# A router softmax on one NeuronCore: the late rows of x loaded in pairs instead of singly

## The chip, the cores and the metric

The kernel runs on one core of one Trainium2 chip. The metric is the time on the device in microseconds (us), the median of several executions. One execution was also taken by the hardware profiler; its span runs from the first to the last instruction or transfer that the profile shows and is a little shorter than the time of that execution.

## The reference

```
logits = matmul(x, router_weights)            # x: 16 x 512 x 1024 fp32, weights: 1024 x 8 fp32
exp_logits = exp(logits - max(logits, -1))    # per token, over 8 values
return exp_logits / sum(exp_logits, -1)       # 16 x 512 x 8 fp32
```

There are 16 x 512 = 8192 tokens of 1024 values each. Every token is multiplied with a 1024 x 8 matrix, and a softmax is taken over its 8 results. Reading x (33.6 MB in fp32) is by far the largest transfer; the output is 0.26 MB.

## The kernel before

The 8192 tokens are laid out as 128 partitions by 64 rows (`J = 64`): partition p holds tokens 64p to 64p+63, so one "row" j is one token in every partition, 128 tokens in all, and several neighbouring rows of one partition are contiguous in memory. A row of x is 128 x 1024 values, 512 KB in fp32.

**Loads.** `LOADS` (line 38) says how many rows each load brings: thirteen loads of four rows, three of two, five of one, which are rows 0 to 62. The first load goes through SyncE in fp32 and is cast by ScalarE. All others are issued by GpSimd (line 76) and cast from fp32 to bf16 on the way, each into a tile of its own, so no load waits for a buffer. The last row, 63, comes in two pieces (`LAST_LOADS = [6, 2]`, line 86): columns 0 to 767 and columns 768 to 1023. All loads issued by GpSimd share one DMA queue and are issued in the order of the rows.

**Work on a row.** The schedule is written out by hand: on each engine the instructions stand in the order of the program (`tc.manual_schedule()`).

- `turn` (line 155) transposes the row's eight 128 x 128 blocks on TensorE into PSUM (line 162). From row `NEAR = 54` on, five blocks go into one PSUM buffer and three into another. There are four such buffers (`psum_t`, line 49).
- `evict` (line 169) copies the transposed blocks to SBUF (line 173): up to row 53 VectorE copies all eight, from row 54 on VectorE copies five and ScalarE three.
- `project` (line 107) multiplies the row's eight blocks with the weights, eight matmuls that accumulate (line 114).
- `softmax` (line 124) puts five small steps on a list (`later`): `peak` (L134), `power` (L137 on VectorE and L140 on ScalarE), `total` (L143), `recip` (L146), `scale` (L149). `GROUPS` says which rows share one softmax; rows 54 to 61 are a group of eight. `step()` takes the next of the five from the list, one after each row.

**The loop** (line 182) runs over rows 0 to 61: it turns and evicts row j, takes one step of a softmax, and projects the row before it (from row 54 on). For rows 24 to 59 one or two filler matmuls (line 104) follow; rows 60 and 61 have none.

**The end** (lines 193 to 224) is written out. Row 61 is projected; the first two softmax steps of the group 54 to 61 run (`peak`, `power`); row 62 is turned and evicted; `total` runs; the two pieces of row 63 are turned, row 62 is projected, row 63 is evicted and projected, and a shared softmax of rows 62 and 63 ends in the last store (line 224):

```
        while pend:
            project(*pend.pop(0))
        step(2)
        xb, k = x_of[J - 2]
        before = evict(turn(xb[:, k, :], (5, 3)))
        step(1)
        (xa, ka, na), (xb, kb, nb) = x_last
        turned = turn(xa, (4, 2), ka) + turn(xb, (2, 0), kb)
        project(J - 2, before)
        last = evict(turned)
```

SyncE stores rows 0 to 53 of the output (line 195) after a tiny transfer (`mark`, line 194) that waits for the first piece of row 63.

Of the kernel before, what the change touches and what calls it, by code (L numbers as in the profile page):

```python
# [10 lines left out]
def kernel(  # L11
# [23 lines left out]
    ALU = mybir.AluOpType  # L35


    LOADS = [4] * 13 + [2, 2, 2] + [1] * 5
    LAST_LOADS = [6, 2]
    GROUPS = [8] * 6 + [6, 8, 1, 1]  # L40
    assert sum(LOADS) == J - 1 and sum(LAST_LOADS) == KO and sum(GROUPS) == J
    DONE = sum(GROUPS[:7])
# [11 lines left out]
    with tc.manual_schedule():  # L54
# [7 lines left out]

        x_f32 = const.tile([P, LOADS[0], D], fp32)
        for k in range(0, LOADS[0], 2):
            nc.sync.dma_start(out=x_f32[:, k:k + 2, :], in_=x_rows[:, k:k + 2, :])
# [3 lines left out]
        j0 = 0  # L69
        for i, r in enumerate(LOADS):  # L70
            xb = xpool.tile([P, r, D], bf16, name=f"x_{i}", tag=f"x_{i}")
# [183 lines left out]
```

## Time and profile before

| What | Value |
|---|---|
| time, median of 3 executions | 88.93 us (88.87 to 88.97) |
| the profiled execution | 88.78 us, its span 87.0 us |
| TensorE transposes and matmuls (PE) | busy 63.8 us, 73% of the span |
| VectorE (DVE) | busy 48.1 us, 55% |
| ScalarE (ACT) | busy 12.4 us, 14% |
| GpSimd (POOL), of which issuing loads 20 x 543 ns and 2 x 527 ns | busy 12.9 us, 15% |
| read from memory | 33.59 MB, written 0.26 MB |
| loads of four rows issued by GpSimd | 12, each 1024 KB as written in bf16 |
| loads of two rows | 3, each 512 KB |
| loads of one row | 5, each 256 KB |
| the pieces of the last row | 192 KB and 64 KB |

In the profile, PE is TensorE's matmuls and transposes, PEld its weight loads, DVE is VectorE, ACT is ScalarE, POOL is GpSimd, SP is SyncE. A line of the timeline reads: start in us from the span's start, duration in us, engine, source line, operation, output and input, number of instructions, and in brackets how long the engine had been idle and what ended that. A line of the chain of waits gives the shares of the span that the chain, followed back from the last instruction, spends on each kind of work. The ends of matmuls are modelled, so starts are read rather than ends where both are there. When GpSimd shows as idle until a DMA, it waits for an earlier load of its own to land before it issues the next.

### The profile page before, as it was taken

The page shows a single profiled execution, that of the slowest core. Times are in us where ns is not written, and L with a number is a line of the kernel's source. Part 1 is how long each engine was busy: PE and PEld are TensorE (multiplying, and loading weights), DVE is VectorE, ACT ScalarE, POOL GpSimd, SP SyncE. Part 2 cuts the span into 40 slices and gives each one's busy share as a digit, 9 for nine tenths or more (in the row PEclk, how much of TensorE's full clock was granted, in tenths as well). Part 3 has the DMA queues.
Part 4 walks back from the last instruction along what each step waited for, and adds up shares of the span by engine and source line. Part 5 has one row for each costly group of instructions (what it writes and reads, how often), then busy time and mean ns, then how long its engine had stood idle before and what let it go on. Part 6 is the DMA issues. An engine that isn't in the chain of part 4 may idle for free.

```text
span 87.0 us, 2427 instructions
## 1 busy us (share of the span) xinstructions
PE 63.8 (73%) x1092; PEld 53.6 (62%) x1092; DVE 48.1 (55%) x112; ACT 12.4 (14%) x25; POOL 12.9 (15%) x29
## 2 busy tenths in 40 slices
PE   0408004999396926949999998989898999997730
PEld 0407004999296926947777775757575888795620
DVE  0303300699576663723677677746676589563760
ACT  3235009000100010000010001000100003454540
POOL 5990002020010202020010202020010222000000
PEclk9999999999956999555999999999999999999997
DMA  3899999999999999999999999999999999999520
GB/s 60 328 358 286 260 249 222 222 211 230 196 222 211 222 215 211 226 207 215 218 215 226 200 226 215 207 226 207 226 207 198 220 213 210 202 210 211 88 102 19
DMA packets 3773, 18.26 MB, mean 210 GB/s; under 512 B 556, under 2 KB 940, under 8 KB 1972
## 3 DMA queue, kind: packets, MB, share of 16 engines
q0 software_dynamic: 3168, 15.73, 88.3%
q1 hardware_dynamic: 580, 2.36, 7.3%
q8 instruction: 8, 0.13, 0.5%
q10 hardware_dynamic: 16, 0.03, 0.2%
q14 instruction: 1, 0.01, 0.0%
HBM read 33.59 MB, written 0.26 MB: 389 GB/s over the span
## 4 chain that ended last, share of the span: by engine, by line
DMA 89%; POOL 3%; issue 2%; DVE 1%; PE 1%; ACT 0%; POOLq 0%
DMA x<-in_x_dram 75%; DMA xe<-in_x_dram 14%; POOL x L76 2%; POOL filler L81 1%; DVE xT L173 0%; PE lg L114 0%; PE pt L162 0%; POOL ident masks.py:199 0%; ACT ev_last L215 0%; POOL ident masks.py:197 0%; DVE ssum_last L219 0%; DVE low L214 0%; DVE ssum_last L220 0%; DVE outv L221 0%; POOLq L239 0%
## 5 line engine op out<-in xcount | busy, mean ns | idle before, releaser
L173 DVE COPY xT<-pt 128x1024 bf16<-128x1024 bf16 (+2 forms) x65 | 42.0, 652 | 31.8 <-PE pt L162 31.6
L162 PE MATMUL pt<-identity,x 128*128 128x128 bf16 x504 | 43.4, 236 | 16.0 <-ACT x L74 8.1
L162 PEld LDWEIGHTS <-x 128*128 128x128 bf16 x504 | 34.6, 105 | 25.8 <-DMA x<-in_x_dram 10.9
L114 PE MATMUL lg<-w_bf,xT 128*128 128x8 bf16 x512 | 22.7, 168 | 0.3 <-DVE xT L173 0.2
L114 PEld LDWEIGHTS <-xT 128*128 128x128 bf16 x512 | 20.7, 99 | 0.5 <-DVE xT L173 0.5
L104 PE MATMUL spare<-filler 128*128 128x512 bf16 x60 | 19.2, 384 | 0.0
L76 POOL DMA_DIRECT2D x<-in_x_dram x20 | 10.7, 543 | 56.2 <-DMA x<-in_x_dram 55.4
L140 ACT ACTIVATE ev<-ex 128x64 f32<-128x64 f32 (+1 forms) x8 | 2.0, 255 | 56.2 <-DVE ex L137 56.2
L173 ACT COPY xT<-pt 128x384 bf16<-128x384 bf16 (+1 forms) x10 | 4.7, 467 | 5.1 <-PE pt L162 4.9
L74 ACT CAST x<-x_f 128x1024 bf16<-128x1024 f32 x4 | 4.0, 1042 | 8.5 <-DMA x_f<-in_x_dram 8.5
L104 PEld LDWEIGHTS <-filler 128*128 128x128 bf16 x60 | 4.1, 96 | 0.0
L92 PE MATMUL lg<-ident,w 8*128 8x8 f32 x8 | 1.0, 254 | 3.1 <-POOL ident masks.py:199 3.1
L92 PEld LDWEIGHTS lg<-ident,w 8*128 8x128 f32 x8 | 1.0, 198 | 3.1 <-POOL ident masks.py:199 3.1
L89 DVE CAST identity<-ident 128x128 bf16<-128x128 f32 x1 | 0.5, 512 | 3.0 <-POOL ident masks.py:199 3.0
L134 DVE TENSOR_REDUCE mx<-lg 128x8 f32<-128x64 f32 (+1 forms) x8 | 1.7, 213 | 0.5 <-PE lg L114 0.5
L137 DVE TENSOR_TENSOR ex<-lg,mx 128x64 f32<-128x64 f32 (+1 forms) x8 | 1.7, 213 | 0.0
L149 DVE TENSOR_TENSOR outv<-ev,inv 128x64 f32<-128x64 f32 (+1 forms) x8 | 1.7, 212 | 0.0
L143 DVE TENSOR_REDUCE ssum<-ev 128x8 f32<-128x64 f32 (+1 forms) x8 | 1.7, 208 | 0.0
L86 POOL DMA_DIRECT2D xe<-in_x_dram x2 | 1.1, 527 | 3.9 <-DMA x<-in_x_dram 3.9
L146 DVE RECIPROCAL inv<-ssum 128x8 f32<-128x8 f32 (+1 forms) x8 | 1.5, 191 | 0.0
L74 ACT ACT_TABLE_LOAD x1 | 1.3, 1283 | 1.3 <-PEq L239 1.3
L162 PE MATMUL pt<-identity,xe 128*128 128x128 bf16 x8 | 0.6, 222 | 0.2 <-DMA xe<-in_x_dram 0.2
(14 smaller groups left out, 3.4 us busy)
## 6 DMA issues: line engine op xcount, KB each, us to landing
x<-in_x_dram POOLq DMA_DIRECT2D x12, 1024.0 KB, 35.4
x_f<-in_x_dram SPq DMA_DIRECT2D x2, 1024.0 KB, 8.4
x<-in_x_dram POOLq DMA_DIRECT2D x3, 512.0 KB, 33.9
x<-in_x_dram POOLq DMA_DIRECT2D x5, 256.0 KB, 20.6
out_dram<-outv SPq DMA_DIRECT2D x1, 216.0 KB, 1.9
xe<-in_x_dram POOLq DMA_DIRECT2D x1, 192.0 KB, 11.8
xe<-in_x_dram POOLq DMA_DIRECT2D x1, 64.0 KB, 9.7
out_dram<-outv SPq DMA_DIRECT2D x1, 40.0 KB, 1.5
```

The source lines that it names most:

```text
L74: nc.scalar.copy(xb[:, k, :], x_f32[:, k, :])
L76: nc.gpsimd.dma_start(out=xb[:], in_=x_rows[:, j0:j0 + r, :])
L92: nc.tensor.transpose(w_ps[:, n, :], w8[:, :, n], ident[0:KO, 0:KO])
L104: nc.tensor.matmul(spare[:], lhsT=filler[:, 0:P], rhs=filler[:], start=True, stop=True)
L114: nc.tensor.matmul(logits[g][:, k, :], lhsT=xT[:, i, :], rhs=w_bf[:, k0 + i, :], start=(k0 + i == 0), stop=(k0 + i == KO - 1),)
L134: nc.vector.reduce_max(mx[:, :, 0], lg, axis=X)
L137: nc.vector.tensor_tensor(out=ex[:], in0=lg, in1=mx[:].broadcast_to([P, n, N]), op=ALU.subtract)
L140: nc.scalar.activation(ev[:], ex[:], func=Exp)
L143: nc.vector.reduce_sum(ssum[:, :, 0], ev[:], axis=X)
L149: nc.vector.tensor_tensor(out=outv[:, a:a + n, :], in0=ev[:], in1=inv[:].broadcast_to([P, n, N]), op=ALU.mult)
L162: nc.tensor.transpose(pt[:, c, :], xb[:, (i + c) * P:(i + c + 1) * P], identity[:])
L173: copy(out=xT[:], in_=pt[:, 0:n, :])
```

## The change

The last eight loads of whole rows before, three of two rows and five of one, become six: five of two rows and one of one row. Rows 52 to 57 come in pairs as they did. Rows 58 and 59, which were two loads, are one; so are rows 60 and 61. Row 62 stays a load of its own, and row 63 stays in its two pieces.

```diff
-    LOADS = [4] * 13 + [2, 2, 2] + [1] * 5
+    LOADS = [4] * 13 + [2] * 5 + [1]
     LAST_LOADS = [6, 2]
     GROUPS = [8] * 6 + [6, 8, 1, 1]
```

GpSimd issues 20 loads instead of 22. The order of the instructions on TensorE, VectorE, ScalarE and SyncE is the same; four rows are read out of tiles that hold two rows.

## The prediction

> **What bounds the kernel now.** I read the page's slices first, then the chain of waits, then GpSimd's timeline for the pace of the loads, and last the timeline of the end, where the edit acts. From the page, the DMA row and the chain by line:
>
> ```profile
> DMA  3899999999999999999999999999999999999520
> ...
> DMA x<-in_x_dram 75%; DMA xe<-in_x_dram 14%; POOL x L76 2%; POOL filler L81 1%; DVE xT L173 0%; PE lg L114 0%; PE pt L162 0%; POOL ident masks.py:199 0%; ACT ev_last L215 0%; POOL ident masks.py:197 0%; DVE ssum_last L219 0%; DVE low L214 0%; DVE ssum_last L220 0%; DVE outv L221 0%; POOLq L239 0%
> ```
>
> The DMA engines are busy from the second slice to slice 37 of 40, and loads are 89% of the chain. So the time is the load stream plus what must be computed after its last piece. The stream's pace, from the timeline of GpSimd:
>
> ```profile
> 62.90 0.53 POOL L76 DMA_DIRECT2D x<-in_x_dram  x1 [4.37 <-DMA x<-in_x_dram]
> 67.81 0.53 POOL L76 DMA_DIRECT2D x<-in_x_dram  x1 [4.38 <-DMA x<-in_x_dram]
> 70.27 0.53 POOL L86 DMA_DIRECT2D xe<-in_x_dram  x1 [1.93 <-DMA x<-in_x_dram]
> 72.72 0.53 POOL L86 DMA_DIRECT2D xe<-in_x_dram  x1 [1.93 <-DMA x<-in_x_dram]
> ```
>
> GpSimd issues eight loads at once and then one for each that lands, so these starts are landings of the loads eight places earlier: 67.81 is the last load of four rows, 70.27 and 72.72 are the first two pairs. Four rows take 4.91 us, two rows 2.46 and 2.45. The last issue comes at 72.72, nearly 10 us before its data is used: the queue never runs dry.
>
> The end, from the timeline of all engines, 77.5 to 83.5 us:
>
> ```profile
> 77.45 0.57 PEld L162 LDWEIGHTS <-x 128*128 128x128 bf16 x8
> ...
> 77.97 0.31 PEld L114 LDWEIGHTS <-xT 128*128 128x128 bf16 x8
> ...
> 78.20 0.10 PEld L104 LDWEIGHTS <-filler 128*128 128x128 bf16 x1
> ...
> 78.70 0.45 PEld L162 LDWEIGHTS <-x 128*128 128x128 bf16 x8 [0.40 <-DMA x<-in_x_dram]
> ...
> 79.97 0.45 PEld L162 LDWEIGHTS <-x 128*128 128x128 bf16 x8 [0.56 <-DMA x<-in_x_dram]
> ...
> 80.38 0.31 PEld L114 LDWEIGHTS <-xT 128*128 128x128 bf16 x8
> ...
> 80.46 0.49 DVE L173 COPY xT<-pt 128x640 bf16<-128x640 bf16 x1 [0.78 <-PE pt L162]
> 80.69 0.48 ACT L173 COPY xT<-pt 128x384 bf16<-128x384 bf16 x1 [0.79 <-PE pt L162]
> 81.01 0.35 PEld L114 LDWEIGHTS <-xT 128*128 128x128 bf16 x8 [0.33 <-DVE xT L173]
> ...
> 81.28 0.46 PEld L162 LDWEIGHTS <-x 128*128 128x128 bf16 x8
> ...
> 81.49 0.23 DVE L134 TENSOR_REDUCE mx<-lg 128x8 f32<-128x64 f32 x1 [0.53 <-PE lg L114]
> ...
> 81.89 0.48 DVE L173 COPY xT<-pt 128x640 bf16<-128x640 bf16 x1
> 82.00 0.26 ACT L140 ACTIVATE ev<-ex 128x64 f32<-128x64 f32 x1 [0.84 <-DVE ex L137]
> ...
> 82.15 0.47 PEld L162 LDWEIGHTS <-xe 128*128 128x128 bf16 x8 [0.41 <-DMA xe<-in_x_dram]
> ...
> 82.17 0.91 ACT L173 COPY xT<-pt 128x384 bf16<-128x384 bf16 x2
> 82.29 0.22 DVE L143 TENSOR_REDUCE ssum<-ev 128x8 f32<-128x64 f32 x1
> ...
> 82.59 0.62 DVE L173 COPY xT<-pt 128x512 bf16<-128x512 bf16 x2
> ```
>
> Counting back from the end, the turns (L162) at 77.45, 78.70, 79.97, 81.28 and 82.15 are rows 59, 60, 61, 62 and 63. Rows 60 and 61 are waited for, 0.40 and 0.56 us, so their landings are 78.70 and 79.97. Two things then meet at 82.59. One is the last row: it lands at 82.15 and is turned. The other starts at row 61: its copy (80.46), its projection (81.01), then on VectorE `peak` (81.49), `power`, the copy of row 62 (81.89) and `total` (82.29 to 82.51), and only then the copy of row 63. That chain is done 0.08 us before it is needed. VectorE often starts an instruction about 0.08 before the one ahead of it ends by the profile (81.89 after an end at 82.37 gives 82.29), so the room is 0.08 to 0.16 us; I take 0.12. The page's chain names the load because it came last, but row 61 is almost level with it.
>
> **What the Trainium skill says.** "DMA: Bandwidth & Descriptors", section "Anatomy of one DMA", gives about 2.0 us fixed per DMA issued by GpSimd, mostly the wait for the receipt of the write. The trace agrees that it is no cost here: with eight in flight, single rows land every 1.25 us (74.97 to 79.97, four rows, below). The same page, section "Why a DMA increments its semaphore by 16 and not by 1", says that a load is complete only when all engines have posted; so neither row of a pair can be used until the whole pair lands. The trace shows it: rows 56 and 57 start at 74.97, after a wait for DMA, and 75.64, without one. "Perfetto Trace Analysis", section "DMA Optimizations", states both sides of the edit: larger transfers use the memory better, and splitting lets work start sooner. The trace has a size for each.
>
> **The change part by part.**
>
> *Two issues removed on GpSimd* (2 x 0.53 us), and the pieces of row 63 issued two places earlier: nothing, since the last issue before already lies some 9.4 us ahead of its landing, behind a full queue. The rest of GpSimd's queue is empty then. SyncE's `mark` still waits for the first piece of row 63, and its store of rows 0 to 53 only follows that piece: nothing.
>
> *The stream becomes a little faster.* From 74.97 (third pair landed) to 79.97 (row 61 landed) four single rows take 5.00 us. Two pairs at 2.455 take 4.91. So row 61 lands 0.09 us earlier, and so do rows 62 and 63. Bounds from the last two single rows, which took 2.52 (77.45 to 79.97), 0.065 more than a pair: 0.06 if only one pair gains that, 0.13 if both do.
>
> *Rows 58 and 59 arrive together* at about 77.45 - 0.05 = 77.40. TensorE is through with row 57 and its filler at about 76.50 and then idles. Two rows cost 0.87 us each with filler (rows in full flow at 69.10 and 69.97 start so), so it is free at about 79.15, before the next pair lands. Nothing, hidden by the wait for rows 60 and 61.
>
> *Rows 60 and 61 arrive together* at 79.97 - 0.09 = 79.88, and row 60's work, before done at 78.70 in the wait for row 61, now stands in front of row 61's. On TensorE that is the turn of row 60 and the projection of row 59: 0.41 us from the turn's first weight load to the projection's (79.97 to 80.38), and 0.23 us from the projection's first weight load to the next instruction (77.97 to 78.20). Bounds 0.64, and 0.71 if the projection's loads must end first (0.41 + 0.30); I take 0.66. VectorE (0.49 per copy) and ScalarE (0.48) keep up with that, and the four PSUM buffers hold exactly these two rows, so no other wait is added. Row 61's turn thus starts at 79.88 + 0.66 = 80.54 instead of 79.97: 0.57 late.
>
> *What is queued behind it.* Row 61's projection is followed in program order by row 62's turn on TensorE, which then starts at 81.85, when row 62 has been there since about 81.1 (79.97 + 1.25 - 0.09); by `peak` and `power` and row 62's copy on VectorE; by the exponential (82.00) and row 62's copy on ScalarE. All move by 0.57. Row 63's turn is no longer held by its load but by row 62's. Of the 0.57, the room of 0.12 at 82.59 is used up; the rest moves row 63's copy, its projection and the last softmax and store one for one.
>
> Sum against the profiled span: 87.0 + 0.66 - 0.09 - 0.12 = 87.45, that is +0.45 us. On the median of the runs, 88.93 (the profiled execution took 88.78, within 0.2% of it), it gives 89.38. With all bounds at one end it is 0.64 - 0.13 - 0.16 = +0.35 and 0.71 - 0.06 - 0.08 = +0.57.
>
> **The rivals.** A change of 0.2%, 0.18 us, is about what a measurement of this kernel can tell from none.
>
> *A: the stream alone sets the end.* If the row-61 chain has more room than I read, the time moves by the stream's gain: 88.93 - 0.09 = 88.84, no measurable change, the other side of my forecast. It decides when the room is at least 0.57 instead of 0.12. For it speaks that the chain of waits names the load; against it, that `total` ends 0.08 before the copy of row 63. A version of it that is faster by over 0.2% needs pairs to gain more than 0.18 us, over the 0.13 bound.
>
> *B: partial absorption.* Row 62's copies and row 63's overlap better when they come densely, and half of the delay is lost on the way: about +0.2, 89.13.
>
> *C: more is added.* If the second row of the pair costs a full row as in full flow (0.87, rows at 69.10 and 69.97), since its turn waits for copies or buffers, the sum is 0.87 - 0.09 - 0.12 = +0.66, 89.59. Against it: rows 60 and 61 have no filler.
>
> That the edit does not do what it says is out: the instruction order shows two loads fewer on GpSimd and the same order elsewhere.
>
> **How the numbers follow.** My forecast, 89.38 with 89.28 to 89.50 of its own, has 0.62; C 0.13, B 0.13 (half of it under the 0.2% line), A 0.12, of which a third is faster by over 0.2% with some luck in the runs. The range from 89.05 to 89.65 takes in most of B and C and leaves out A. Faster 0.04, within 0.2% 0.15 (0.08 of A and 0.07 of B), slower 0.81.
>
> **What would show it.** Right: TensorE's turn of row 60 near 79.9 with a wait for DMA ahead of it, row 61's turn about 0.65 later without one; `peak` of the last group near 82.05 instead of 81.49; the turn of row 63 no longer waiting for its load; the last store near 85.1 instead of 84.62; landings of pairs every 2.45 us to the end. Wrong: row 63's turn still waiting for its load at about 82.06 and the last store before 84.7 (A), or row 61's turn 0.87 after row 60's (C).

## The result, and the profile after

| | before | after |
|---|---|---|
| time, median | 88.91 us (88.74 to 88.97, 6 executions) | 89.12 us (89.04 to 89.27, 6 executions) |
| span of the profiled execution | 87.0 us | 87.5 us |

The ratio is 1.0029, with a 95% interval of 1.0016 to 1.0042: the changed kernel is slower, by 0.26 us (0.14 to 0.37); the two medians alone differ by 0.21. A second measurement gave 1.0032 (1.0020 to 1.0043), which is 0.28 us. The forecast was 0.45 us slower, so the direction is right and the size too large. The profiled execution of the changed kernel was the slowest of its six (89.27), that of the kernel before is below its median (88.78), so the two spans differ by more than the medians do.

The page of the changed kernel, its DMA row and the chain by line:

```profile
DMA  2999999999999999999999999999999999999220
...
DMA x<-in_x_dram 89%; PE lg L114 1%; PE pt L162 1%; DVE xT L173 1%; ACT ev_last L215 0%; DVE mx L134 0%; DVE ex L137 0%; DVE ssum_last L219 0%; DVE low L214 0%; DVE ssum_last L220 0%; DVE outv L221 0%; POOLq L239 0%
```

The stream is as busy as before, but the chain no longer ends with the pieces of row 63 (xe, 14% before). It runs over a load of whole rows and then over `peak` and `power` (L134, L137), which were not on it. The timeline of the end, all engines:

```profile
77.49 0.45 PEld L162 LDWEIGHTS <-x 128*128 128x128 bf16 x8 [0.84 <-DMA x<-in_x_dram]
...
78.16 0.65 PEld L162 LDWEIGHTS <-x 128*128 128x128 bf16 x8
...
79.95 0.45 PEld L162 LDWEIGHTS <-x 128*128 128x128 bf16 x8 [0.85 <-DMA x<-in_x_dram]
...
80.35 0.31 PEld L114 LDWEIGHTS <-xT 128*128 128x128 bf16 x8
...
80.44 0.49 DVE L173 COPY xT<-pt 128x640 bf16<-128x640 bf16 x1 [0.99 <-PE pt L162]
80.59 0.45 PEld L162 LDWEIGHTS <-x 128*128 128x128 bf16 x8
...
81.09 0.49 DVE L173 COPY xT<-pt 128x640 bf16<-128x640 bf16 x1 [0.16 <-PE pt L162]
...
81.63 0.35 PEld L114 LDWEIGHTS <-xT 128*128 128x128 bf16 x8 [0.30 <-DVE xT L173]
...
81.91 0.46 PEld L162 LDWEIGHTS <-x 128*128 128x128 bf16 x8
...
82.11 0.23 DVE L134 TENSOR_REDUCE mx<-lg 128x8 f32<-128x64 f32 x1 [0.53 <-PE lg L114]
82.15 0.71 SPq L194 DMA_DIRECT2D mark<-xe  x1
82.33 0.43 PEld L162 LDWEIGHTS <-xe 128*128 128x128 bf16 x7
...
82.92 0.22 DVE L143 TENSOR_REDUCE ssum<-ev 128x8 f32<-128x64 f32 x1
83.05 0.27 PE L162 MATMUL pt<-identity,xe 128*128 128x128 bf16 x2 [0.17 <-DVE xT L173]
...
83.06 0.61 DVE L173 COPY xT<-pt 128x512 bf16<-128x512 bf16 x2
...
85.07 0.34 SPq L224 DMA_DIRECT2D out_dram<-outv  x1
```

The turns at 77.49, 78.16, 79.95, 80.59, 81.91 and 82.33 are rows 58 to 63. Each pair is waited for once: the first row has a wait for DMA, the second has none. Row 60's turn starts where row 61's did (79.95, before 79.97), and row 61's follows 0.64 us later. `peak` starts at 82.11 instead of 81.49. SyncE's `mark` shows when the first piece of row 63 is there: 82.15, before 82.13. Yet row 63's weight loads, at 82.33, no longer name a wait for it. The last store starts at 85.07 instead of 84.62. The two lines of the kernel before:

```profile
82.13 0.70 SPq L194 DMA_DIRECT2D mark<-xe  x1
...
84.62 0.34 SPq L224 DMA_DIRECT2D out_dram<-outv  x1
```

To compare executions whose streams run some tenths earlier or later, I count from GpSimd's start after the landing of the last load of four rows (67.81 in the kernel before). It is the last landing which the edit does not touch and which GpSimd's starts show in both kernels. In the changed kernel it is the issue of the second piece of row 63:

```profile
67.90 0.53 POOL L86 DMA_DIRECT2D xe<-in_x_dram  x1 [4.32 <-DMA x<-in_x_dram]
```

So 0.09 us of the 0.45 between the two last stores is only that this execution's stream ran later. "To mark", "to peak" and "to store" below mean the starts of L194, of the last L134 and of the last store, counted from there.

### The profile page after: what moved, and what is told of

It is laid out like the page before. It is cut to its first block, busy times and chain, and to the rows that moved or that the text cites. A ratio compares the mean times of both kernels' runs of the same rounds, so it can differ in the third digit from the quotient of the medians.

```text
span 87.5 us, 2413 instructions
## 1 busy us (share of the span) xinstructions
PE 62.0 (71%) x1080; PEld 52.8 (60%) x1092; DVE 48.0 (55%) x112; ACT 12.3 (14%) x25; POOL 11.8 (14%) x27
## 4 chain that ended last, share of the span: by engine, by line
DMA 89%; PE 3%; DVE 2%; issue 2%; ACT 0%; POOLq 0%
DMA x<-in_x_dram 89%; PE lg L114 1%; PE pt L162 1%; DVE xT L173 1%; ACT ev_last L215 0%; DVE mx L134 0%; DVE ex L137 0%; DVE ssum_last L219 0%; DVE low L214 0%; DVE ssum_last L220 0%; DVE outv L221 0%; POOLq L239 0%
## 5 line engine op out<-in xcount | busy, mean ns | idle before, releaser
L162 PE MATMUL pt<-identity,x 128*128 128x128 bf16 x504 | 42.8, 234 | 17.7 <-DMA x<-in_x_dram 9.5
L162 PEld LDWEIGHTS <-x 128*128 128x128 bf16 x504 | 34.0, 104 | 27.1 <-DMA x<-in_x_dram 13.3
L76 POOL DMA_DIRECT2D x<-in_x_dram x18 | 9.7, 545 | 48.2 <-DMA x<-in_x_dram 47.5
L104 PE MATMUL spare<-filler 128*128 128x512 bf16 x48 | 15.5, 377 | 0.6
L134 DVE TENSOR_REDUCE mx<-lg 128x8 f32<-128x64 f32 (+1 forms) x8 | 1.7, 214 | 0.5 <-PE lg L114 0.5
L137 DVE TENSOR_TENSOR ex<-lg,mx 128x64 f32<-128x64 f32 (+1 forms) x8 | 1.7, 213 | 0.0
```

Source lines behind the costliest of these rows:

```text
L76: nc.gpsimd.dma_start(out=xb[:], in_=x_rows[:, j0:j0 + r, :])
L104: nc.tensor.matmul(spare[:], lhsT=filler[:, 0:P], rhs=filler[:], start=True, stop=True)
L134: nc.vector.reduce_max(mx[:, :, 0], lg, axis=X)
L137: nc.vector.tensor_tensor(out=ex[:], in0=lg, in1=mx[:].broadcast_to([P, n, N]), op=ALU.subtract)
L162: nc.tensor.transpose(pt[:, c, :], xb[:, (i + c) * P:(i + c + 1) * P], identity[:])
```

## The experiments

**The two halves of the change, and the whole again.** Rows 58 and 59 alone as a pair (first edit), rows 60 and 61 alone as a pair (second edit), and the changed kernel as it is.

```diff
-    LOADS = [4] * 13 + [2, 2, 2] + [1] * 5
+    LOADS = [4] * 13 + [2] * 4 + [1] * 3
```

> Only rows 58 and 59 come as a pair; rows 60, 61 and 62 stay single. Theory (row 60's work stands in front of row 61's): no loss, since TensorE waits for row 60 anyway; the stream gains about 0.05 us, so between 0.1 us less and 0.05 us more than before, and in the trace row 61's turn starts when its load lands, with peak of the last group near 81.45. Rival (a pair costs by itself, wherever it stands): about half of the measured 0.21 us, so 0.1 us more. Rival (the stream gains more than 0.09 us): 0.15 us less or better.

```diff
-    LOADS = [4] * 13 + [2, 2, 2] + [1] * 5
+    LOADS = [4] * 13 + [2, 2, 2] + [1, 1, 2, 1]
```

> Only rows 60 and 61 come as a pair; rows 58 and 59 stay single. Theory: all of the loss is here, and it is some 0.05 us larger than that of the whole change, because one pair's gain in the stream is missing: 0.25 to 0.5 us more than before; row 61's turn 0.65 us after row 60's. Rival (a pair costs by itself): half of the change, 0.1 us more.

> The changed kernel again, on the same chip as its two halves. The sum worked out in the prediction is 0.45 us more than before, the first measurement gave 0.21. If the sum is right and the first runs were scattered, 0.35 to 0.5 us more; if part of the delay is lost in most executions, 0.15 to 0.3 us again, and a trace in which the landing of the last whole rows comes earlier or later by some tenths than in the first one.

| Pair at rows | median, us | before beside it | ratio, 95% interval |
|---|---|---|---|
| 58 and 59 | 88.86 | 88.92 | 0.9988 (0.9975 to 1.0001) |
| 60 and 61 | 89.47 (89.11 to 89.96) | 88.92 | 1.0064 (1.0043 to 1.0086) |
| both, the change | 89.25 | 88.92 | 1.0032 (1.0020 to 1.0043) |

The whole loss belongs to rows 60 and 61. The timeline of the kernel with rows 58 and 59 as a pair shows why the other half is free:

```profile
79.15 0.65 PEld L162 LDWEIGHTS <-x 128*128 128x128 bf16 x8
...
80.12 0.45 PEld L162 LDWEIGHTS <-x 128*128 128x128 bf16 x8
...
81.64 0.23 DVE L134 TENSOR_REDUCE mx<-lg 128x8 f32<-128x64 f32 x1 [0.53 <-PE lg L114]
...
82.31 0.71 SPq L194 DMA_DIRECT2D mark<-xe  x1
...
82.33 0.45 PEld L162 LDWEIGHTS <-xe 128*128 128x128 bf16 x8 [0.44 <-DMA xe<-in_x_dram]
...
84.79 0.34 SPq L224 DMA_DIRECT2D out_dram<-outv  x1
```

Row 60's turn (79.15) no longer waits for its load, as TensorE is still at work on the pair ahead of it. But row 61's turn, at 80.12, is not late: it starts 12.10 us after the landing (68.02 in this trace) against 12.16 before. `peak` is 0.67 ahead of `mark` (0.64 before), and row 63 is waited for as before. The store comes at 84.79 - 68.02 = 16.77 us against 16.81. Whether that small gain is real the interval leaves open.

The pair at rows 60 and 61 alone costs more than the whole change, and its executions lie between 89.11 and 89.96. That was not foreseen. Stretches of a microsecond of its profiled execution, with TensorE's granted clock (1.00 is full) ahead of the DMA share, and some lines of its timeline:

```profile
core 0: us, PE busy (x) PEld busy (x) DVE busy (x) ACT busy (x) POOL busy (x), PEclk, DMA share, GB/s
...
79.00:80.00 1.00, 0.00 (x0) 0.00 (x0) 0.00 (x0) 0.03 (x1) 0.00 (x0) 1.00 1.05 196
...
82.00:83.00 1.00, 1.00 (x17) 1.00 (x17) 0.53 (x3) 0.15 (x2) 0.00 (x0) 0.50 0.04 4
```

```profile
80.19 0.45 PEld L162 LDWEIGHTS <-x 128*128 128x128 bf16 x8 [1.62 <-DMA x<-in_x_dram]
...
82.17 0.77 PEld L162 LDWEIGHTS <-x 128*128 128x128 bf16 x8
...
82.37 0.22 DVE L134 TENSOR_REDUCE mx<-lg 128x8 f32<-128x64 f32 x1 [0.54 <-PE lg L114]
...
85.80 0.34 SPq L224 DMA_DIRECT2D out_dram<-outv  x1
```

TensorE idles 1.62 us for the pair, and some 1.7 us after it resumes its clock is at 0.50: the eight weight loads of row 62 take 0.77 us instead of 0.46. The store comes 3.43 us after `peak`; in the changed kernel it is 2.96 (82.11 to 85.07), and there, with waits of 0.84 and 0.85 us, the clock stayed at 1.00 to the last projection. This profiled execution is the slowest of the ten. Five of them took 89.11 to 89.30 us, the other five 89.63 to 89.96.

**The clock as the cause of that extra.** The same pair, with fillers in the wait:

```diff
-    LOADS = [4] * 13 + [2, 2, 2] + [1] * 5
+    LOADS = [4] * 13 + [2, 2, 2] + [1, 1, 2, 1]
...
                 fill(2 if j < 48 else 1)
+            if j == 59:
+                fill(6)
```

> Only rows 60 and 61 as a pair, with six more filler matmuls on TensorE after row 59, which end by about 79.9 in the wait for the pair and compute nothing that is used. If the slow executions with the pair at rows 60 and 61 alone come from TensorE's idling of 1.6 us, after which its clock fell to half, the fillers keep the clock up and the time is 0.3 to 0.45 us more than before, with little spread, instead of 0.55 with 0.85 between the fastest and the slowest. Rival (the clock falls whatever TensorE does): the same spread as without fillers.

89.35 us (89.17 to 89.47) against 88.98, ratio 1.0039 (1.0026 to 1.0052). From its timeline:

```profile
80.11 0.45 PEld L162 LDWEIGHTS <-x 128*128 128x128 bf16 x8 [0.52 <-DMA x<-in_x_dram]
...
82.08 0.46 PEld L162 LDWEIGHTS <-x 128*128 128x128 bf16 x8
...
82.28 0.23 DVE L134 TENSOR_REDUCE mx<-lg 128x8 f32<-128x64 f32 x1 [0.53 <-PE lg L114]
...
85.24 0.34 SPq L226 DMA_DIRECT2D out_dram<-outv  x1
```

The spread fell from 0.85 to 0.30 us, and the difference of the medians from 0.55 to 0.37. `peak` comes as long after the landing as without fillers (14.26 us, 14.27 without), but row 62's weight loads take 0.46 us again, and the store is 2.96 after `peak`. So the extra came from the clock, and keeping TensorE busy in the wait removed it. (The two were run on different chips, each beside the kernel before.) What is left is the cost of the pair itself: 0.35 us (0.23 to 0.46) by the ratio, which these intervals do not tell from that of the whole change.

**A late row 61 without a change of loads.** Five fillers hold up TensorE between rows 60 and 61:

```diff
                 fill(2 if j < 48 else 1)
+            if j == 60:
+                fill(5)
```

> The loads of before, with five more filler matmuls on TensorE after the projection of row 59, ahead of row 61's turn; they compute nothing that is used. No load changes. Five at 0.21 us each, from about 79.4, end at 80.46 by the trace of before, so row 61's turn starts 0.49 us late. Theory (a late row 61 costs, less a room of 0.12 us): 0.37 us more than before by the sum, and not under 0.2. Rival (the loss of the change comes from how its loads land, and the load of row 63 sets the end): no change.

89.16 us against 88.92, ratio 1.0021 (1.0009 to 1.0033). Its timeline (the edit moves later lines by two):

```profile
80.44 0.65 PEld L162 LDWEIGHTS <-x 128*128 128x128 bf16 x8
...
82.16 0.23 DVE L134 TENSOR_REDUCE mx<-lg 128x8 f32<-128x64 f32 x1 [0.53 <-PE lg L114]
...
82.36 0.71 SPq L196 DMA_DIRECT2D mark<-xe  x1
...
85.12 0.34 SPq L226 DMA_DIRECT2D out_dram<-outv  x1
```

Not one load differs from the kernel before, and a good part of the loss is there: 0.19 us (0.08 to 0.29) by the ratio, which is half of the 0.37 expected and just under the 0.2 given as the least. The trace has 0.28, as follows. `peak` is 0.20 ahead of `mark` instead of 0.64, so 0.44 us late; the store is 2.76 after `mark` instead of 2.49, so 0.27 late. The difference, 0.17 us, is the room. (Counted from the landing, the store comes at 17.10 us against 16.82 before.)

**Less work in front of row 61.** The changed kernel, with row 59 projected in the wait for the pair:

```diff
-    LOADS = [4] * 13 + [2, 2, 2] + [1] * 5
+    LOADS = [4] * 13 + [2] * 5 + [1]
...
                 fill(2 if j < 48 else 1)
+            if j == 59:
+                project(*pend.pop(0))
```

> The changed kernel, with the projection of row 59 moved ahead of row 60's turn, into TensorE's wait for the pair. Theory (what stands in front of row 61's turn costs): row 61's turn starts 0.41 us after row 60's instead of 0.65, so 0.24 us of the loss goes: 0.0 to 0.1 us more than before. Rival (the copies on VectorE and ScalarE, 0.49 us each row, hold row 61 then): 0.08 us of the loss stays, 0.1 to 0.2 us more than before. Rival (the order on TensorE does not matter): 0.2 to 0.35 us more, as the changed kernel.

88.99 us against 88.98, ratio 0.9997 (0.9982 to 1.0011), that is 0.03 us less (0.16 less to 0.10 more): no loss is left that the measurement can tell. Its timeline:

```profile
79.50 0.35 PEld L114 LDWEIGHTS <-xT 128*128 128x128 bf16 x8 [0.30 <-DVE xT L173]
...
80.05 0.90 PEld L162 LDWEIGHTS <-x 128*128 128x128 bf16 x16 [0.21 <-DMA x<-in_x_dram]
...
80.55 0.94 DVE L173 COPY xT<-pt 128x640 bf16<-128x640 bf16 x2 [0.99 <-PE pt L162]
...
82.02 0.23 DVE L134 TENSOR_REDUCE mx<-lg 128x8 f32<-128x64 f32 x1 [0.53 <-PE lg L114]
82.25 0.71 SPq L196 DMA_DIRECT2D mark<-xe  x1
...
84.98 0.34 SPq L226 DMA_DIRECT2D out_dram<-outv  x1
```

The two rows are now turned in one block of sixteen, and the copies follow each other without a gap. From the landing of the pair to `peak` it is 1.97 us (80.05 to 82.02) instead of 2.16: 0.19 won, not 0.24, which fits VectorE's copies of 0.47 each (0.94 for two) having become the pace, the first rival. In this one trace the store is still 16.97 us from the landing, 0.15 above the kernel before. So the trace shows 0.20 of the 0.35 us removed, while the runs show all of it removed; 0.15 lies outside their interval. The trace is where the first rival put it (0.1 to 0.2 more than before), the runs are where the theory did (0.0 to 0.1). Both say that the order on TensorE matters; they do not agree on how much is left.

**A larger dose.** Rows 61 and 62 as the pair:

```diff
-    LOADS = [4] * 13 + [2, 2, 2] + [1] * 5
+    LOADS = [4] * 13 + [2, 2, 2] + [1, 1, 1, 2]
```

> Rows 61 and 62 come as the pair, all others as before. Theory: row 61 is now usable only when row 62 lands, 1.25 - 0.05 = 1.20 us later than before, and nothing hides it but the room, which the traces so far put at 0.17 us: 1.0 us more than before, up to 0.5 more on top where TensorE's clock drops in the wait. Rival (a pair costs by itself): 0.1 us. Rival (the landing of row 63 sets the end): none.

90.20 us against 88.98, ratio 1.0142 (1.0109 to 1.0174). Its timeline:

```profile
81.15 0.77 PEld L162 LDWEIGHTS <-x 128*128 128x128 bf16 x8 [1.77 <-DMA x<-in_x_dram]
...
82.07 0.71 SPq L194 DMA_DIRECT2D mark<-xe  x1
...
82.89 0.77 PEld L162 LDWEIGHTS <-x 128*128 128x128 bf16 x8
83.09 0.23 DVE L134 TENSOR_REDUCE mx<-lg 128x8 f32<-128x64 f32 x1 [0.69 <-PE lg L114]
...
86.53 0.34 SPq L224 DMA_DIRECT2D out_dram<-outv  x1
```

Row 61 waits for row 62's data and starts at 81.15 instead of 79.97. The load of row 63 is as early as ever (82.07), and the end is far behind it. This profiled execution took 90.69 us, and its clock is halved (0.77 for eight loads again). The other three, not profiled, took 90.03 to 90.32, which is 1.05 to 1.34 above the median before; whether the clock fell in them too is not known. By the ratio the loss is 1.26 us (0.97 to 1.55), within what was expected with and without the clock.

**The price of single loads in the stream.** Rows 40 to 62 singly, 13 loads more; the last rows are as before:

```diff
-    LOADS = [4] * 13 + [2, 2, 2] + [1] * 5
+    LOADS = [4] * 10 + [1] * 23
```

> Rows 40 to 62 all come singly, 13 loads more than before; the last rows' order and sizes are as before. This prices small loads in the stream alone. By the pace in the trace of before, 1.25 us for a single row against 1.2275 in fours and pairs, 18 more single rows cost 18 x 0.0225 = 0.4 us. Rival (a load's fixed cost of a microsecond or two shows somewhere): several us. Rival (the number of loads costs nothing, only bytes do): no change.

89.52 us against 88.98, ratio 1.0075 (1.0046 to 1.0104). GpSimd's timeline, from the landing of the last load of four rows in this kernel (rows 36 to 39):

```profile
53.16 0.53 POOL L76 DMA_DIRECT2D x<-in_x_dram  x1 [4.40 <-DMA x<-in_x_dram]
54.40 0.53 POOL L76 DMA_DIRECT2D x<-in_x_dram  x1 [0.71 <-DMA x<-in_x_dram]
55.61 0.53 POOL L76 DMA_DIRECT2D x<-in_x_dram  x1 [0.69 <-DMA x<-in_x_dram]
56.86 0.53 POOL L76 DMA_DIRECT2D x<-in_x_dram  x1 [0.73 <-DMA x<-in_x_dram]
```

In the kernel before, the same load lands at 53.16 too. `mark` is at 82.67 here and at 82.13 there: 0.54 us for 18 more single rows, 0.030 us each. The same stretch takes 28.97 to 29.12 us in four traces of the kernel before (three of them follow below) and 29.51 here, so 0.02 to 0.03 us each is as much as one trace can say; the runs have 0.67 us (0.41 to 0.93) in all. Single rows thus cost the stream a little, in line with the gain that the change was credited with, and no fixed cost of a microsecond or more per load shows.

**More traces of the two kernels, unchanged.** One execution each.

> The kernel before once more, for its trace alone. The sum from the traces (0.65 later on TensorE, 0.08 gained in the stream, 0.17 of room, so 0.40 us more) is about 0.1 us above the measured ratios. Theory 1: the executions only scatter ahead of the end, and every trace of the kernel before shows about 14.32 us from the landing of its last load of four rows to SyncE's mark, and 2.49 us from mark to the last store. Theory 2: in many executions of the kernel before the first piece of row 63 lands late, which it pays for in full and the changed kernel does not; then this trace shows 14.4 or more.

> As for the other further trace of the kernel before: 14.32 and 2.49 us by theory 1, 14.4 or more to mark by theory 2.

> As for the other further traces of the kernel before: 14.32 and 2.49 us by theory 1, 14.4 or more to mark by theory 2.

> The changed kernel once more, for its trace alone: 14.24 us from the landing of the last load of four rows to mark, 2.16 from the landing of row 61 to peak, 2.96 from peak to the last store. Theory 2 would show in a late mark here too, with the last store still 2.96 after peak.

They took 89.06, 88.80, 88.86 and 89.11 us; one execution of the kernel before beside them took 88.95. Together with the earlier traces, all in us, worked out from the starts in each timeline:

| Trace | landing to row 61's data | landing to mark | landing to peak | mark to store | peak to store | landing to store |
|---|---|---|---|---|---|---|
| before | 12.16 | 14.32 | 13.68 | 2.49 | 3.13 | 16.81 |
| before, second | 12.15 | 14.33 | 13.67 | 2.49 | 3.15 | 16.82 |
| before, third | 12.16 | 14.33 | 13.68 | 2.49 | 3.14 | 16.82 |
| before, fourth | 12.16 | 14.33 | 13.67 | 2.49 | 3.15 | 16.82 |
| after | 12.05 | 14.25 | 14.21 | 2.92 | 2.96 | 17.17 |
| after, second | 12.11 | 14.48 | 14.28 | 2.76 | 2.96 | 17.24 |
| after, third | 12.04 | 14.23 | 14.21 | 2.93 | 2.95 | 17.16 |
| five fillers | | 14.34 | 14.14 | 2.76 | 2.96 | 17.10 |
| pair 60 and 61, six fillers | 12.09 | 14.28 | 14.26 | 2.94 | 2.96 | 17.22 |
| pair 58 and 59 | | 14.29 | 13.62 | 2.48 | 3.15 | 16.77 |
| less work in front of row 61 | 12.04 | 14.24 | 14.01 | 2.73 | 2.96 | 16.97 |
| pair 60 and 61, clock halved | 12.09 | 14.28 | 14.27 | 3.42 | 3.43 | 17.70 |
| pair 61 and 62, clock halved | 13.37 | 14.29 | 15.31 | 4.46 | 3.44 | 18.75 |

Two columns carry the study. Where row 63's load comes last, the store is 2.48 or 2.49 after `mark`; where row 61's chain does, it is 2.95 or 2.96 after `peak`, as long as the clock is at 1.00. The end is the later of the two, and they are level when `peak` is 2.96 - 2.49 = 0.47 ahead of `mark`. In the kernel before it is 0.64 to 0.66 ahead, so there is 0.17 to 0.19 of room. Theory 2 finds no support: in none of the four traces of the kernel before does row 63's piece land late, though four traces do not rule it out for a smaller part of the executions. It did land late in one trace of the changed kernel (14.48), and there it cost nothing, since row 61's chain was behind it anyway.

## Why the prediction was right, and where its size was off

**What bounds the kernel.** Right, including the part that the page's chain did not show: the load of row 63 came last, and row 61's chain was almost level with it. The chain of the changed kernel goes over `peak` and `power`, and five fillers alone, with no load changed, bring a loss of the same kind (0.28 of 0.35 us in the traces).

**GpSimd's two issues fewer, and SyncE's store.** Nothing, as forecast. The pieces of row 63 were issued at 63.05 and 67.90 instead of 70.27 and 72.72, and the first landed at about the same time: 14.25, 14.48 and 14.23 us from the landing, before 14.32 and 14.33.

**Rows 58 and 59 hidden.** Right: rows 58 and 59 as a pair alone cost nothing that shows. The prediction took the turn of row 59 at 77.45 as its landing, though that turn names no wait; the pair landed at 77.49, which is 77.40 on the time of the kernel before, as forecast.

**The gain of the stream**, 0.09: right in kind and about in size. From the last load of four rows, row 61's data comes 0.11, 0.05 and 0.12 us earlier in the three traces of the changed kernel.

**Row 60's work in front of row 61's**, 0.66: 0.64 in the trace (79.95 to 80.59), at the low bound. Taking a part of that work away removed the loss in the runs and 0.20 of 0.35 us in the trace.

**The room**, 0.12: too small, the term that was furthest off. It is 0.17 to 0.19. When the chain runs without a pause, VectorE's copy of row 63 starts 0.14 us after the start of `total` (82.92 to 83.06) and so 0.08 before `total` ends by the profile; in the kernel before it starts 0.30 after it (82.29 to 82.59). The difference is 0.16, the upper of the prediction's two bounds (0.08 and 0.16), between which it took the middle. From the copy to the store it is another 0.02 less (2.01 us, before 2.03).

The sum with these sizes is 0.64 - 0.11 - 0.17 = 0.36. Two traces of the changed kernel give 0.34 to 0.36 (17.16 and 17.17 less 16.81 or 16.82), and the second one 0.42, where row 61's data came only 0.05 us earlier. The sum of 0.45 was thus about 0.1 too large through three terms that all erred to the same side, each within or just outside its bound. That the last store was forecast near 85.1 and came at 85.07 is in part luck, as that execution's stream ran 0.09 later.

The runs say less still. Their 0.26 us (0.14 to 0.37) and 0.28 (0.18 to 0.38) hold 0.35 near the upper ends. The median of 89.12 is under the 89.28 to 89.50 that the prediction gave its own sum, and inside the wider range of 89.05 to 89.65, which took in most of rival B. The runs lie below the traces in four of the experiments too: 0.19 against 0.28 us with five fillers, 0.35 against 0.40 with rows 60 and 61 as a pair and six fillers, 0.03 less than before against 0.15 more with less work in front of row 61, 0.11 less against 0.05 less with rows 58 and 59 as a pair. With single rows in the stream they lie above, 0.67 against 0.54. What makes this gap, if it is more than scatter, stays open.

**The rivals.** A, the stream alone: fell, as the room is 0.17 and not 0.57. B, partial absorption, +0.2: the measured 0.26 and 0.28 us lie between it and the forecast, and nearer to it. Its mechanism does not show in the traces: what they have is the larger room, not half of the delay lost in a denser overlap, since from `peak` on every trace with the late row 61 and the full clock takes the same 2.95 or 2.96. For executions without a trace it is not ruled out. C, a full row of 0.87: fell, the second row follows after 0.64.

**A wait not foreseen.** I wrote that the PSUM buffers add none. For rows 60 and 61 that holds. But row 63's second piece needs a buffer that row 62 still fills, and TensorE waits for VectorE's copy (83.05, 0.17 us). It is inside the 2.96 and did not make what follows the copy longer: from VectorE's copy of row 63 to the second `low` step (L214) it is 0.91 us, before 0.92.

## What to carry to other kernels

In this kernel, joining two loads near the end of the stream makes the stream faster by hundredths of a microsecond and holds the first of the two back until the second lands. Price it by the work that then stands in front of the last row on the computing engine, less the room of the chain that this row starts. A chain of waits names only the path that came last: look for the path that is nearly level with it, and test it by delaying it with work that computes nothing. Where the delay is hidden in a wait that comes anyway, as for rows 58 and 59, a pair is free.

## What was not expected of the hardware

TensorE's clock dropped to 0.50, with work still to do, in the traces where it had waited 1.62 and 1.77 us for a pair, and not in that of the changed kernel with waits of 0.84 and 0.85 us. In the first of them it fell near 81.8, some 1.6 us after the wait had ended; in the second near 80.95, still within the wait. With the pair at rows 60 and 61 alone the executions spread over 0.85 us, and six fillers in the wait brought that to 0.30. In the trace with rows 60 and 61 paired, the store came 3.43 us after `peak` instead of 2.96: half a microsecond from a wait that had already ended.

The length of a wait alone does not tell when the clock falls. In the trace with rows 58 and 59 as a pair, where TensorE's weight loads had waited no longer than 0.65 us at a time since 68 us, it fell near 83.8, just after TensorE's last projection and too late to cost anything. What sets the moment is not shown by these runs.
